# Left halves of three normalized residuals turned by transposing DMAs instead of TensorE

## The chip, the cores and the metric

The kernel runs on one core of a Trainium2 chip. The metric is the time of one execution in device microseconds (us); the time before is the median of three runs. The engines are named as in the profile: PE (TensorE, matrix products and transposes), PEld (its weight loads), DVE (VectorE), ACT (ScalarE), POOL (GpSimd) and SP (SyncE, which only issues DMAs here).

## The reference

One decoder layer on 256 tokens of width 2048, in float32. `h` is the residual stream:

```
h = h + 0.5 * swiglu(rmsnorm(h, g_ffn1), w1_gate, w1_up, w1_down)      # "f1", width 5632
z = rmsnorm(h, g_mix) @ w_in                                           # q, kv, v, u
y = concat(rmsnorm(spatial_gating(z)), rmsnorm(window_attention(z)))
h = h + y @ w_out                                                      # "wo"
h = h + cross_attention(rmsnorm(h, g_x), rmsnorm(mem, g_mem), ...)     # "xq", ..., "xo"
h = h + 0.5 * swiglu(rmsnorm(h, g_ffn2), w2_gate, w2_up, w2_down)      # "f2"
return rmsnorm(h, g_final)

def rmsnorm(x, g):
    return x * rsqrt(mean(x * x) + 1e-5) * g
```

Three of these norms stand between a product that adds into `h` and the next product: n2 (g_mix), n3 (g_x) and n4 (g_ffn2). They are the ones that change.

## The kernel before

**Products.** `h` lies by rows: 256 tokens are two blocks of 128 partitions, and the 2048 columns are four parts (j = 0 to 3) of 512. A product with a weight matrix needs the left operand turned, so that the 128 partitions hold columns. For this the columns are cut into eight pairs of 128 columns each; pair i holds two column blocks by two token blocks, a tile of 128 x 512. The "left half" of a norm is parts j = 0 and 1, pairs 0 to 3.

Each float32 product is done in three passes: an operand is split into a high half (a cast on ACT, line 147) and a low half (the rest, a subtraction on DVE, line 148), and PE multiplies high by high, low by high and high by low (line 411). Products of 2 x 2 blocks are done in a form with seven products instead of eight; the kinds "C", "S" and "D" of a pair say which sums and differences of its blocks `fill` makes on DVE (the tiles named f, for instance n2f).

**Units and chunks.** A unit is one product of all pairs with 1024 columns of a weight matrix; it runs chunk by chunk, one pair with one megabyte of weights each. `load` brings the weights by SP (three buffers for what comes in, two for the halves) and splits them: f1dw, f1dwh and f1dwl are the weights of the unit f1d, their high and their low half. Kind "S" also makes sums of weight blocks (f1dt).

**The order.** PE runs in the order in which the program is written. The other engines' instructions are put in order by a scheduler when the kernel is built; on the chip each engine takes its list strictly in that order. Small work beside the products is written as generators in the list `side`: after every sixth matmul `side_step` lets one of them go on, and the number that a generator yields is how many such steps it then rests.

**The norms.** `next_norm` returns `on_block`, which the unit that adds into `h` calls for each block that is done. The squares of a block are summed on ACT (line 137, output junk). When the left half is there, an estimated factor from its squares scales the rows (`scaled`, line 822, tile n2s, n3s or n4s); the right parts are scaled by the same factor once they are done, after the last chunk of the unit. `make` then turns pair after pair: `transposed` makes four PE transposes into a PSUM bank (tile n, line 231), two ACT instructions per pair read the bank and multiply by the norm's gain g (line 249, tile n2r), and `fill` makes the differences and the halves (n2fh, n2fl). Its generators rest 4 steps before the first pair of a part and 1 before the second.

**Additions into h.** A unit of wo or xo ends with a group of additions on DVE (lines 610 to 624, early sums, and 604, the last four). They stand between the low halves of the last chunks in DVE's list.

**A way of turning that is already there.** In the feed-forward parts the rows are turned without PE: `rows_done` copies the rows on ACT so that the low and the high halfwords of the floats lie apart (line 661, tile f1w), SP issues a transposing DMA on 16-bit elements (line 665, tile f1a), and `joined` puts the halfwords together again, two ACT copies per pair (line 679, tile f1r).

Of the kernel before, what the change touches and what calls it, by code (L numbers as in the profile page):

```python
# [10 lines left out]
U16 = mybir.dt.uint16  # L11
AF = mybir.ActivationFunctionType
# [3 lines left out]
P = 128  # L16
T = 256
TB = 2
# [15 lines left out]
def layer_kernel(  # L34
# [22 lines left out]
    nc = tc.nc  # L57
# [26 lines left out]
    sm = const.tile([P, N_SMALL], F32, name="sm")  # L84
# [34 lines left out]
    h = const.tile([P, TB, D], F32, name="h")  # L119


    def rstd_of(parts, n, width, nt=TB):

        ss = tiny.tile([P, nt], F32, tag="ss", name=nm("ss"))
        if n > 1:
            nc.vector.tensor_reduce(out=ss, in_=parts, axis=AX.X, op=ALU.add)
        else:
            ss = parts.rearrange("p t n -> p (t n)")
        ms = tiny.tile([P, nt], F32, tag="ms", name=nm("ms"))
        nc.vector.tensor_scalar(ms, ss, 1.0 / width, EPS, op0=ALU.mult, op1=ALU.add)  # L130
        rs = tiny.tile([P, nt], F32, tag="rs", name=nm("rs"), bufs=8)
        nc.gpsimd.tensor_tensor(rs, ms, mhalf[:, :nt], ALU.pow)
        return rs

    def square_into(parts_ap, src, width):
        junk = s2("junk")
        nc.scalar.activation(junk[:, :width], src, AF.Square, accum_out=parts_ap)

    def split_scaled(hi, lo, src, g):

        nc.scalar.activation(hi, src, AF.Copy, scale=g)
        nc.vector.scalar_tensor_tensor(
            out=lo, in0=src, scalar=g, in1=hi.bitcast(F32), op0=ALU.mult, op1=ALU.subtract
        )

    def split(hi, lo, src):
        nc.scalar.copy(hi, src)  # L147
        nc.vector.tensor_tensor(lo, src, hi.bitcast(F32), ALU.subtract)  # L148

    def products(o, passes):  # L150
        for i, (a, b) in enumerate(passes):
            nc.tensor.matmul(o, a, b, start=i == 0, stop=i == len(passes) - 1)
# [49 lines left out]
    def fill(s, p, raw):  # L202

        f = s2(s + "f").rearrange("p (k t) -> p k t", k=4)
        if p.kind == "C":
            f = f[:, :2, :]
            nc.vector.tensor_tensor(f, raw[:, 0:2, :], raw[:, 2:4, :], ALU.subtract)
        elif p.kind in "SD":
            nc.vector.tensor_tensor(
                f[:, 0:2, :], raw[:, 0:1, :].to_broadcast([P, 2, P]), raw[:, 1:3, :], ALU.subtract  # L210
            )
        split(p.base[0], p.base[1], raw)
        if p.kind in "SD":
# [12 lines left out]
    def transposed(s, kind, src):  # L226

        ps = bank(s).rearrange("p (k t) -> p k t", k=4)
        for k in range(2):
            for tb in range(TB):  # L230
                nc.tensor.transpose(ps[:, laid(kind, k, tb), :], src(tb, k), ident)
        return ps

    def row_tile(kind, v, k):

        return v[:, k::2, :] if kind == "C" else v[:, 2 * k:2 * k + 2, :]

    def pair_from_rows(s, kind, src, gcol):
        ps = transposed(s, kind, src)
        p = Pair(s, kind)  # L240
        if kind != "N":
            raw = s2(s + "r").rearrange("p (k t) -> p k t", k=4)
        for k in range(2):
            g = sm[:, gcol + k:gcol + k + 1]
            if kind == "N":
                hi, lo = [row_tile("N", t, k) for t in p.base]
                split_scaled(hi, lo, row_tile("N", ps, k), g)
            else:
                nc.scalar.activation(row_tile(kind, raw, k), row_tile(kind, ps, k), AF.Copy, scale=g)
        if kind != "N":  # L250
            fill(s, p, raw)
        return p
# [171 lines left out]
    def side_add(gen):  # L424
        side.append([now[0], gen])
# [226 lines left out]
    def ffn(s, get, rs, wgu, wd, on_block, first=None, on_token_block=None):  # L652
        acts = [None] * 22
        pairs = [None] * 22

        def rows_done(c, rows_):
            turned_ = m4(s + "a").bitcast(U16).rearrange("p (b c t) -> p b c t", b=TB, c=8)

            def turned(tb):
                w = s2(s + "w").bitcast(U16)  # L660
                nc.scalar.copy(
                    w.rearrange("p (h c) -> p h c", h=2),
                    rows_[tb].bitcast(U16).rearrange("p (c h) -> p h c", h=2),
                )
                nc.sync.dma_start_transpose(turned_[:, tb], w)
                for q in range(2):
                    acts[2 * c + q] = turned_

            for tb in range(TB):
                later.append((tb, lambda tb=tb: turned(tb)))  # L670

        def joined(i):
            turned_ = have(acts, i).rearrange("p b (h c) t -> p b c t h", h=2)
            raw = s2(s + "r")
            words = raw.bitcast(U16).rearrange("p (i t h) -> p i t h", i=4, h=2)
            q = 2 * (i % 2)
            for tb in range(TB):
                j, k = laid(KINDS_D[i], 0, tb), laid(KINDS_D[i], 1, tb)
                nc.scalar.copy(words[:, j:k + 1:k - j], turned_[:, tb, q:q + 2])
            return raw.rearrange("p (i t) -> p i t", i=4)  # L680
# [76 lines left out]
        for n, idx in enumerate(turns):  # L757
            half = n % 2
            kinds = "".join(KINDS_D[i] for i in idx)
# [28 lines left out]
    def next_norm(s, gcol, kinds="NNNNNNNN"):  # L788

        mixed = "S" in kinds
        parts = tiny.tile([P, TB, NG], F32, tag="parts", name=nm("parts"))
        pairs = [None] * 8
        done = [0] * NG
        st = {}

        def on_block(j, tb):  # L800
            square_into(parts[:, tb, j:j + 1], h[:, tb, j * 512:(j + 1) * 512], 512)
            done[j] += 1
            if not mixed:
                if done[j] == TB:
                    make(j, lambda tb, c: h[:, tb, c:c + P])
            elif j < 2:
                if done[0] + done[1] == 2 * TB:
                    st["est"] = rstd_of(parts[:, :, :2], 2, 1024)

                    def first():  # L810
                        yield 1
                        for i in range(2):
                            scaled(i)

                    side_add(first())
            elif done[j] == TB:
                scaled(j)

        def scaled(j):
            r = m4(s + "s").rearrange("p (b c) -> p b c", b=TB)  # L820
            for tb in range(TB):
                nc.scalar.activation(
                    r[:, tb], h[:, tb, j * 512:(j + 1) * 512], AF.Copy, scale=st["est"][:, tb:tb + 1]
                )
            make(j, lambda tb, c: r[:, tb, c - j * 512:c - j * 512 + P])

        def make(j, src):
            def work():
                for i in (2 * j, 2 * j + 1):
                    yield 4 if i % 2 == 0 and mixed else 1  # L830
                    pairs[i] = pair_from_rows(
                        s, kinds[i], lambda tb, k: src(tb, (2 * i + k) * P), gcol + 2 * i
                    )

            side_add(work())

# [531 lines left out]
    for j in range(2):  # L1368
        g = m4("gf")
# [123 lines left out]
```

## Time and profile before

| | us |
|---|---|
| median of the runs | 2039.45 (2039.23, 2039.45, 2040.15) |
| the profiled execution | 2038.53 |
| its span, first to last instruction | 2036.8 |
| PE busy | 2019.8 (99%) |
| DVE busy | 1858.2 (91%) |
| ACT busy | 1297.9 (64%) |
| mean granted clock of PE | 0.998 |

The profile is of one execution, so sums over its rows are compared with 2038.53 and not with the median. Times in a trace are counted from the start of the span. The f1d unit ends and q begins near 701; wo ends and xq begins near 1138; xo ends and f2g begins near 1342. A row of a timeline gives start, length, engine, line, operation, output<-input; in brackets stands how long the engine was idle before and what released it. "x2" joins equal neighbours.

### The profile page before, as it was taken

To read this page: it belongs to the slowest core of one execution; us is meant where nothing else is said; L and a number is where in the kernel's file an instruction comes from. 1 tells how busy PE (TensorE), PEld (TensorE's weight loads), DVE (VectorE), ACT (ScalarE), POOL (GpSimd) and SP (SyncE) were. 2 spreads that over 40 slices of the span, in tenths; PEclk is the share of its full clock that TensorE was granted. 3 is DMA by queue.
4 is the path that set the end of the run, shared out by engine and by line. 5 is a ranking of instruction groups with operands and counts; after the bars stand their busy time and mean duration, and the time that the engine had idled before them with its cause. 6 is when DMAs were issued, how large, how long until landed. Compare 5 with 4: busy or idle time off the path is not lost.

```text
span 2036.8 us, 24300 instructions
## 1 busy us (share of the span) xinstructions
PE 2019.8 (99%) x9235; PEld 1671.6 (82%) x9235; DVE 1858.2 (91%) x1998; ACT 1297.9 (64%) x1432; POOL 36.3 (2%) x57
## 2 busy tenths in 40 slices
PE   9999999999999999999999999999999999999998
PEld 8788888888888888888888888888888888888886
DVE  6999999999999978988988987899999999999998
ACT  7865656567665766655556655675656666676664
POOL 0000000000000010100000000000000000000000
PEclk9999999999999999999999999999999999999999
DMA  8666666666555565545555544556566656665563
GB/s 312 195 209 232 214 219 197 232 217 218 204 192 205 187 243 176 196 166 183 193 182 179 198 161 145 186 186 218 199 234 210 217 213 225 220 215 209 186 225 127
DMA packets 106884, 413.72 MB, mean 203 GB/s; under 512 B 53376, under 2 KB 55440, under 8 KB 59664
## 3 DMA queue, kind: packets, MB, share of 16 engines
q1 hardware_dynamic: 104320, 405.04, 57.5%
q0 software_dynamic: 2016, 6.30, 0.9%
q8 instruction: 72, 1.18, 0.2%
q10 hardware_dynamic: 432, 0.84, 0.1%
q14 instruction: 44, 0.36, 0.1%
HBM read 398.52 MB, written 2.10 MB: 197 GB/s over the span
## 4 chain that ended last, share of the span: by engine, by line
PE 85%; DVE 8%; issue 3%; ACT 1%; DMA 1%; SPq 0%; POOL 0%; POOLq 0%; DVEq 0%; ACTq 0%
PE f2gQ L411 13%; PE f1gQ L411 12%; PE f2dQ L411 6%; PE f1dQ L411 6%; PE f1gP L411 5%; PE f2gP L411 4%; PE xqQ L411 3%; PE f2dP L411 3%; PE f1dP L411 3%; PE woQ L411 2%; PE xoQ L411 2%; PE f2dR L411 2%; PE f1dR L411 2%; DVE f1gwl L148 2%; PE vQ L411 2%
## 5 line engine op out<-in xcount | busy, mean ns | idle before, releaser
L148 DVE TENSOR_TENSOR f1gwl<-f1gw,f1gwh 128x1536 fp32r<-128x1536 f32 (+2 forms) x94 | 181.6, 1934 | 23.3 <-ACT f1gwh L147 22.4
L147 ACT CAST f2gwh<-f2gw 128x1536 fp32r<-128x1536 f32 (+1 forms) x88 | 150.3, 1711 | 59.6 <-PE f2gQ L411 39.2
L148 DVE TENSOR_TENSOR f2gwl<-f2gw,f2gwh 128x1536 fp32r<-128x1536 f32 (+1 forms) x88 | 179.2, 2037 | 9.6 <-ACT f2gwh L147 9.6
L147 ACT CAST f1gwh<-f1gw 128x1536 fp32r<-128x1536 f32 (+2 forms) x94 | 153.0, 1629 | 44.4 <-PE f1gQ L411 18.0
L147 ACT CAST f1gth<-f1gt 128x1024 fp32r<-128x1024 f32 x76 | 79.9, 1051 | 102.7 <-DVE f1gt L320 67.7
L147 ACT CAST f2gth<-f2gt 128x1024 fp32r<-128x1024 f32 x82 | 85.9, 1049 | 69.7 <-DVE f2gt L324 40.4
L411 PE MATMUL f2gQ<-f2gwh,n4fh 128*128 128x512 f32 x317 | 124.2, 392 | 1.5 <-DVE f2gv L570 1.5
L411 PE MATMUL f2gQ<-f2gwh,n4fl 128*128 128x512 f32 x317 | 123.4, 389 | 0.0
L411 PE MATMUL f1gQ<-f1gwh,n1fl 128*128 128x512 f32 x286 | 111.4, 390 | 1.7 <-DVE n1fl L148 1.7
L411 PE MATMUL f1gQ<-f1gwh,n1fh 128*128 128x512 f32 x286 | 111.6, 390 | 0.0
L147 ACT CAST f2dwh<-f2dw 128x2048 fp32r<-128x2048 f32 (+1 forms) x44 | 77.4, 1759 | 47.5 <-PE f2dQ L411 39.5
L147 ACT CAST f1dwh<-f1dw 128x2048 fp32r<-128x2048 f32 (+1 forms) x44 | 77.3, 1757 | 43.7 <-PE f1dQ L411 42.7
L148 DVE TENSOR_TENSOR f1dwl<-f1dw,f1dwh 128x2048 fp32r<-128x2048 f32 (+1 forms) x44 | 92.0, 2091 | 11.3 <-ACT f1dwh L147 11.2
L148 DVE TENSOR_TENSOR f2dwl<-f2dw,f2dwh 128x2048 fp32r<-128x2048 f32 (+1 forms) x44 | 92.1, 2092 | 11.2 <-ACT f2dwh L147 11.1
L148 DVE TENSOR_TENSOR f2gtl<-f2gt,f2gth 128x1024 fp32r<-128x1024 f32 x82 | 99.7, 1219 | 1.0
L411 PE MATMUL f2gQ<-f2gwl,n4fh 128*128 128x512 f32 x317 | 96.7, 389 | 0.0
L148 DVE TENSOR_TENSOR f1gtl<-f1gt,f1gth 128x1024 fp32r<-128x1024 f32 x76 | 92.2, 1217 | 0.5
L411 PE MATMUL f1gQ<-f1gwl,n1fh 128*128 128x512 f32 x286 | 86.9, 389 | 0.0
L411 PEld LDWEIGHTS f2gQ<-f2gwh,n4fh 128*128 128x128 f32 x317 | 59.5, 188 | 15.9 <-DVE f2gv L570 3.7
L411 PEld LDWEIGHTS f2gQ<-f2gwl,n4fh 128*128 128x128 f32 x317 | 59.4, 188 | 12.3
L411 PEld LDWEIGHTS f2gQ<-f2gwh,n4fl 128*128 128x128 f32 x317 | 59.5, 188 | 12.1
L411 PE MATMUL f2gP<-f2gwh,n4fh 128*128 128x512 f32 x176 | 68.6, 390 | 0.0
(823 smaller groups left out, 6057.8 us busy)
## 6 DMA issues: line engine op xcount, KB each, us to landing
f2gw<-in_w_gu SPq DMA_DIRECT2D x88, 1024.0 KB, 5.1
f1gw<-in_w_gu SPq DMA_DIRECT2D x86, 1024.0 KB, 4.9
f1dw<-in_w_down SPq DMA_DIRECT2D x44, 1024.0 KB, 4.8
f2dw<-in_w_down SPq DMA_DIRECT2D x44, 1024.0 KB, 4.8
wow<-in_w_out SPq DMA_DIRECT2D x16, 1024.0 KB, 4.8
xqw<-in_w_xq SPq DMA_DIRECT2D x16, 1024.0 KB, 4.8
xow<-in_w_xo SPq DMA_DIRECT2D x16, 1024.0 KB, 4.8
qw<-in_w_in SPq DMA_DIRECT2D x8, 1024.0 KB, 4.8
```

What stands on the lines that cost most here:

```text
L147: nc.scalar.copy(hi, src)
L148: nc.vector.tensor_tensor(lo, src, hi.bitcast(F32), ALU.subtract)
L411: nc.tensor.matmul(self.banks[name], x, y, start=name not in self.begun, stop=self.left[name] == 0)
```

## The change

For parts j = 0 and 1 of n2, n3 and n4 the scaled rows are turned in the way of the feed-forward parts. `turned_rows` is called once for each of the two token blocks: one ACT copy of 128 x 1024 halfwords (n2w) and one transposing DMA on SP into n2t; four of each per norm. `pair_joined` takes the place of `pair_from_rows` for pairs 0 to 3: two ACT copies of halfwords from n2t into n2r, two ACT multiplications by g that read and write n2r, then `fill` as before. The generators now rest 6 steps before the first pair of a part and 3 before the second. Parts 2 and 3, and the norms of the feed-forward parts, stay as they are; the hunk that is left out only moves lines of `rows_done` and `joined` into the new helper functions.

```
--- before.py
+++ after.py
@@ -147,6 +147,23 @@
         nc.scalar.copy(hi, src)
         nc.vector.tensor_tensor(lo, src, hi.bitcast(F32), ALU.subtract)
 
+    def turned_rows(s, dst, src):
+
+        w = s2(s + "w").bitcast(U16)
+        nc.scalar.copy(
+            w.rearrange("p (h c) -> p h c", h=2), src.bitcast(U16).rearrange("p (c h) -> p h c", h=2)
+        )
+        nc.sync.dma_start_transpose(dst, w)
+
+    def tile_turned(s):
+        return m4(s).bitcast(U16).rearrange("p (b c t) -> p b c t", b=TB, c=8)
+
+    def by_block(turned):
+        return turned.rearrange("p b (h c) t -> p b c t h", h=2)
+
+    def words_of(raw, n):
+        return raw.bitcast(U16).rearrange("p (i t h) -> p i t h", i=n, h=2)
+
     def products(o, passes):
         for i, (a, b) in enumerate(passes):
             nc.tensor.matmul(o, a, b, start=i == 0, stop=i == len(passes) - 1)
@@ -247,6 +264,27 @@
                 split_scaled(hi, lo, row_tile("N", ps, k), g)
             else:
                 nc.scalar.activation(row_tile(kind, raw, k), row_tile(kind, ps, k), AF.Copy, scale=g)
+        if kind != "N":
+            fill(s, p, raw)
+        return p
+
+    def pair_joined(s, kind, turned, c, gcol):
+
+        raw = s2(s + "r")
+        words = words_of(raw, 4)
+        for tb in range(TB):
+            j, k = laid(kind, 0, tb), laid(kind, 1, tb)
+            nc.scalar.copy(words[:, j:k + 1:k - j], by_block(turned)[:, tb, c:c + 2])
+        raw = raw.rearrange("p (k t) -> p k t", k=4)
+        p = Pair(s, kind)
+        for k in range(2):
+            g = sm[:, gcol + k:gcol + k + 1]
+            src = row_tile(kind, raw, k)
+            if kind == "N":
+                hi, lo = [row_tile("N", t, k) for t in p.base]
+                split_scaled(hi, lo, src, g)
+            else:
+                nc.scalar.activation(src, src, AF.Copy, scale=g)
         if kind != "N":
             fill(s, p, raw)
         return p
...
@@ -822,7 +855,20 @@
                 nc.scalar.activation(
                     r[:, tb], h[:, tb, j * 512:(j + 1) * 512], AF.Copy, scale=st["est"][:, tb:tb + 1]
                 )
-            make(j, lambda tb, c: r[:, tb, c - j * 512:c - j * 512 + P])
+            if j < 2:
+                t = tile_turned(s + "t")
+                for tb in range(TB):
+                    turned_rows(s, t[:, tb], r[:, tb])
+
+                def work():
+                    for q in range(2):
+                        yield 6 if q == 0 else 3
+                        i = 2 * j + q
+                        pairs[i] = pair_joined(s, kinds[i], t, 2 * q, gcol + 2 * i)
+
+                side_add(work())
+            else:
+                make(j, lambda tb, c: r[:, tb, c - j * 512:c - j * 512 + P])
 
         def make(j, src):
             def work():
```

The change moves instructions on ACT and DVE. Three places follow, each before and then now; a number behind a name only tells the tiles of one name apart.

ACT, the end of f1d, where the left half of n2 is scaled. Before:

```order
L147 CAST f1dwh_5246<-f1dw_5245 128x2048
L822 ACTIVATE n2s_5267<-h,rs_5243 128x512 x2
L822 ACTIVATE n2s_5270<-h,rs_5243 128x512 x2
L147 CAST f1dwh_5286<-f1dw_5285 128x1536
L147 CAST f1dth_5299<-f1dt_5289 128x1024
```

and now (line 822 has become 855):

```order
L147 CAST f1dwh_5246<-f1dw_5245 128x2048
L855 ACTIVATE n2s_5267<-h,rs_5243 128x512 x2
L153 COPY n2w_5271<-n2s_5267 128x1024
L153 COPY n2w_5274<-n2s_5267 128x1024
L855 ACTIVATE n2s_5277<-h,rs_5243 128x512 x2
L153 COPY n2w_5281<-n2s_5277 128x1024
L153 COPY n2w_5284<-n2s_5277 128x1024
L147 CAST f1dwh_5300<-f1dw_5299 128x1536
```

Four copies to n2w stand between the scaled rows and the cast of f1d's next weights.

ACT, the end of f1d and the start of q (n2r_5465, n2r_5486 and n2r_5511 are the joined pairs 0, 2 and 1; n2t_5270 holds pairs 0 and 1, n2t_5280 pairs 2 and 3). Before:

```order
L822 ACTIVATE n2s_5583<-h,rs_5243 128x512
L137 ACTIVATE junk_5575,parts_118<-h 128x512
L137 ACTIVATE junk_5578,parts_118<-h 128x512
L137 ACTIVATE junk_5581,parts_118<-h 128x512
L822 ACTIVATE n2s_5583<-h,rs_5243 128x512
L137 ACTIVATE junk_5587,parts_118<-h 128x512
L822 ACTIVATE n2s_5589<-h,rs_5243 128x512 x2
L147 CAST n2fh_5516<-n2f_5521 128x512
L147 CAST qwh_5593<-qw_5592 128x2048
L147 CAST qwh_5631<-qw_5630 128x2048
```

and now:

```order
L147 CAST n2fh_5470<-n2f_5474 128x256
L277 COPY n2r_5486<-n2t_5280 128x512
L147 CAST qwh_5595<-qw_5594 128x2048
L287 ACTIVATE n2r_5486<-n2r_5486,sm 128x2x128 x2
L147 CAST qth_5748<-qt_5742 128x1024
L147 CAST n2fh_5489<-n2r_5486 128x512
L147 CAST qwh_5633<-qw_5632 128x2048
L147 CAST n2fh_5470<-n2f_5493 128x256
L277 COPY n2r_5511<-n2t_5270 128x512 x2
L147 CAST qth_5752<-qt_5742 128x1024
L287 ACTIVATE n2r_5511<-n2r_5511,sm 128x2x128 x2
L147 CAST n2fh_5514<-n2r_5511 128x512
```

Pairs 0 to 3 were made ahead of the first of these rows before, except for one cast of pair 3. Now the last scaled rows (n2s) stand ahead of the first row shown, pair 2 is joined before pair 1, and pair 1's high half (n2fh_5514) is the last row, behind two casts of q's weights.

DVE, the end of wo. Before:

```order
L148 TENSOR_TENSOR wowl_9116<-wow_9114,wowh_9115 128x2048
L621 TENSOR_TENSOR h<-h,wop_1818_9141 128x512
L148 TENSOR_TENSOR wowl_9155<-wow_9153,wowh_9154 128x2048
L611 SCALAR_TENSOR_TENSOR wov_9142<-woQ_1806_9050,wop_1818_9141 128x512
L604 SCALAR_TENSOR_TENSOR h<-woQ_1804_9048,h 128x512
L614 SCALAR_TENSOR_TENSOR woz_9143<-woQ_1805_9049,wov_9142 128x512
L604 SCALAR_TENSOR_TENSOR h<-woQ_1804_9048,h 128x512
L622 TENSOR_TENSOR h<-h,wov_9142 128x512
L623 TENSOR_TENSOR h<-h,woz_9143 128x512
L624 TENSOR_TENSOR h<-h,woz_9143 128x512
```

and now (lines 604, 611, 614 and 621 to 624 have become 642, 649, 652 and 659 to 662):

```order
L148 TENSOR_TENSOR wowl_9088<-wow_9086,wowh_9087 128x2048
L649 SCALAR_TENSOR_TENSOR wov_9114<-woQ_1798_9022,wop_1810_9113 128x512
L642 SCALAR_TENSOR_TENSOR h<-woQ_1796_9020,h 128x512
L652 SCALAR_TENSOR_TENSOR woz_9115<-woQ_1797_9021,wov_9114 128x512
L642 SCALAR_TENSOR_TENSOR h<-woQ_1796_9020,h 128x512
L659 TENSOR_TENSOR h<-h,wop_1810_9113 128x512
L660 TENSOR_TENSOR h<-h,wov_9114 128x512
L661 TENSOR_TENSOR h<-h,woz_9115 128x512
L662 TENSOR_TENSOR h<-h,woz_9115 128x512
L148 TENSOR_TENSOR wowl_9127<-wow_9125,wowh_9126 128x2048
```

The low half of wo's last chunk (wowl_9155, now wowl_9127) stood in front of seven additions and now stands behind them. At the end of xo the low half of the last chunk has moved in the same way, behind eight additions and two rows of pair 2 of n4; and on ACT the loading of a function table (line 93) has moved from before the last squares of n4 to just before the cast of f2g's second chunk.

More of the change, by code (lines that the diff above doesn't have):

```diff
@@ L656, in rows_done @@
         def rows_done(c, rows_):
-            turned_ = m4(s + "a").bitcast(U16).rearrange("p (b c t) -> p b c t", b=TB, c=8)
+            t = tile_turned(s + "a")
             def turned(tb):
[L660 to L665, printed above, removed]
+                turned_rows(s, t[:, tb], rows_[tb])
                 for q in range(2):
-                    acts[2 * c + q] = turned_
+                    acts[2 * c + q] = t
             for tb in range(TB):
@@ L672, in joined @@
         def joined(i):
-            turned_ = have(acts, i).rearrange("p b (h c) t -> p b c t h", h=2)
+            turned_ = by_block(have(acts, i))
             raw = s2(s + "r")
-            words = raw.bitcast(U16).rearrange("p (i t h) -> p i t h", i=4, h=2)
+            words = words_of(raw, 4)
             q = 2 * (i % 2)
```

## The prediction

> **What bounds the kernel now.** I read the busy shares and the chain of waits first.
>
> ```profile
> PE 2019.8 (99%) x9235; PEld 1671.6 (82%) x9235; DVE 1858.2 (91%) x1998; ACT 1297.9 (64%) x1432; POOL 36.3 (2%) x57
> PE 85%; DVE 8%; issue 3%; ACT 1%; DMA 1%; SPq 0%; POOL 0%; POOLq 0%; DVEq 0%; ACTq 0%
> ```
>
> PE sets the time: 2019.8 of 2036.8 us. So a transpose taken from PE is worth its length, and work given to ACT (64% busy) looks free. These are averages over stages, though. Next I read what PE waits for, and the chain of waits where f1d ends and q begins:
>
> ```profile
> PE f1gQ L411 <- DVE n1fl L148: 1.7, 1, 1.7
> ...
> PE xoQ L411 <- ACT n4r L249: 1.2, 1, 1.2
> ```
>
> ```profile
> 692.82 0.44 PE n L231 x4
> ...
> 694.23 1.93 ACT qwh L147
> ...
> 703.50 1.23 ACT n2s L822 x2
> ...
> 707.10 1.20 PE qP L411 x4
> ```
>
> PE waits once for 1.7 us and once for 1.2 (columns: in total, times, longest), and no DMA stands among its waits. But at the junction the chain leaves PE: from 694 to 707 it runs over ACT and DVE. ACT's load there:
>
> ```profile
> 700.00:720.00 20.00, 19.81 (x96) 16.10 (x95) 19.03 (x31) 20.00 (x37) 5.46 (x7) 1.00 0.64 228
> 1095.00:1165.00 70.00, 70.00 (x326) 57.97 (x325) 64.59 (x79) 51.71 (x73) 2.24 (x2) 1.00 0.53 183
> ```
>
> (Columns after the window: its length, then busy us of PE, PEld, DVE, ACT, POOL; then the granted clock.) For 20 us at the start of q ACT is busy all the time. That is where the change puts work on it. The next junction (wo to xq, second row) has room on ACT, 51.71 of 70, but DVE is 92% busy; the third (xo to f2g) is built like it.
>
> **What is removed.** Twelve groups of four transposes, four groups in each of three norms. A group costs PE 0.44 us in the chain above: 12 x 0.44 = **-5.3 us**, all on PE's path. One sentence of the Trainium skill bears on that price. Its page "VectorE: DVE Perf Modes", section "The three transpose paths", gives a 128x128 TensorE transpose 390 ns; taken as a pitch, 48 of them would be -18.7 and the sum below near no change, but the trace puts four in 0.44, so the trace's price stands.
>
> **What is added on ACT.** Per norm four copies that sort halfwords (128x1024) and eight that join a pair (128x512). The first trace shows the same forms in the feed-forward part. In scaling, eight instructions that read PSUM become eight that read SBUF; that form is not shown, so I keep L249's length, and as bounds 0.1 less or more each, 0.8 a norm.
>
> ```profile
> L661 ACT COPY f1w<-f1gz 128x1024 uint16<-128x1024 uint16 x10 | 10.4, 1041 | 0.0
> L679 ACT COPY f1r<-f1a 128x512 uint16<-128x512 uint16 x44 | 27.7, 680 | 0.0
> 709.99 0.82 ACT L249 ACTIVATE n2r<-n,sm 128x256 f32<-128x256 f32 x2
> ```
>
> Successive ACT instructions overlap: two of L249 take 0.82, and a cast of 1.04 is followed 0.95 later by the next (the rows of 710.71 and 711.65 below). I take 0.95 for the first copy and 0.63 for the second: 4 x 0.95 + 8 x 0.63 = 8.8 us of ACT per norm, 26.5 in all. What matters is what stands behind them.
>
> **Junction 1a, in f1d.** The four large copies stand before the cast of an f1d chunk (first place shown of the change).
>
> ```profile
> 669.33 1.46 ACT L147 CAST f1dwh<-f1dw 128x1536 fp32r<-128x1536 f32 x1
> 670.83 1.76 DVE L148 TENSOR_TENSOR f1dwl<-f1dw,f1dwh 128x1536 fp32r<-128x1536 f32 x1 [2.19 <-ACT f1dwh L147]
> ...
> 674.93 0.40 PE L411 MATMUL f1dP<-f1dwl,f1afh 128*128 128x512 f32 x1
> ```
>
> The cast moves from 669.33 to 673.1, its end to 674.6, the low half's end to 676.4. PE, two transpose groups earlier, wants it at 674.93 - 0.88 = 674.05. **+2.4.** Queued behind are the other f1d casts, which have room: two L249 pairs are gone there. With all four groups of n2 gone (1.76), PE is then 0.65 late.
>
> **Junction 1b, q's second chunk.** The pairs come in the order 0, 2, 1, 3, so pair 1, which PE needs second, stands behind pair 2's rows and two casts of q's weights (second place shown).
>
> ```profile
> 701.51 0.69 DVE L604 SCALAR_TENSOR_TENSOR h<-f1dQ,h 128x512 f32<-128x512 f32 x1
> 701.31 0.39 PE L411 MATMUL qP<-qwh,n2fh 128*128 128x512 f32 x1
> 705.14 3.72 ACT L147 CAST qwh<-qw 128x2048 fp32r<-128x2048 f32 x2
> 710.71 1.04 ACT L147 CAST qth<-qt 128x1024 fp32r<-128x1024 f32 x1
> 711.65 0.62 ACT L147 CAST n2fh<-n2r 128x512 fp32r<-128x512 f32 x1
> ...
> 711.83 1.22 DVE L148 TENSOR_TENSOR qtl<-qt,qth 128x1024 fp32r<-128x1024 f32 x1
> ```
>
> The last addition into h ends at 702.20 and now at 702.85; the last scaled rows follow it (0.71) to 703.6. Then ACT does, in the new order, at these lengths less the overlap: 0.31 + 0.63 + 1.86 + 0.74 + 0.95 + 0.53 + 1.86 + 0.31 + 1.26 + 0.95 + 0.74 + 0.62 = 10.8. Pair 1's high half is there at 714.4. PE starts q at 701.31 + 0.65 and ends its first chunk, 24 matmuls at 0.227, at 707.4. **+7.0.** (A cast of 128x256 I put at half of one of 128x512.) Pair 1's low half stands on DVE behind the low half qtl (1.22), some **+1.3** more; the gap that stood there before, from 706.75 to the 707.10 of the chain, is inside the new one: **-0.35**. Junction 1: **+10.4**.
>
> **Junctions 2 and 3, the last wo and xo chunks.** There DVE makes the chunk's low half after the additions into h instead of before (third place shown).
>
> ```profile
> L231 PE MATMUL n<-ident,n3s x16: 270/272/273, 1103.4 to 1109.2; 128*128 128x128 f32 x16
> ...
> 1126.49 2.28 DVE L148 TENSOR_TENSOR wowl<-wow,wowh 128x2048 fp32r<-128x2048 f32 x1
> 1128.69 0.68 DVE L611 SCALAR_TENSOR_TENSOR wov<-woQ,wop 128x512 f32<-128x512 f32 x1
> 1132.29 0.68 DVE L624 TENSOR_TENSOR h<-h,woz 128x512 f32<-128x512 f32 x1
> 1132.93 0.39 PE L411 MATMUL woP<-wowl,ybfh 128*128 128x512 f32 x1
> 1330.70 2.28 DVE L148 TENSOR_TENSOR xowl<-xow,xowh 128x2048 fp32r<-128x2048 f32 x1
> 1337.07 0.39 PE L411 MATMUL xoP<-xowl,xofh 128*128 128x512 f32 x1
> ```
>
> Seven additions from 1128.69 are 7 x 0.60 = 4.2 us; the low half, ready at 1128.77, had 4.16 of room. So the order alone takes all the room and no more. DVE is late by more: PE skips the four groups of the first row (16 transposes up to 1109.2), 1.8 us, ahead of this place, while DVE has the same rows to do. With 0.4 for the copies I take **+2.3** (0 to 4.7: nothing, or 0.9 and the full 3.8 of the large copies on top). For xo two rows of pair 2 (0.28 and 0.6) stand in front too: 5.0 + 2.2 - 4.1 = **+3.1** (0 to 5.6).
>
> Then the next unit's second chunk. Its cast on ACT stands behind the squares and the scaled rows:
>
> ```profile
> 1135.69 0.67 DVE L604 SCALAR_TENSOR_TENSOR h<-woQ,h 128x512 f32<-128x512 f32 x1
> 1137.66 0.61 ACT L137 ACTIVATE junk<-h 128x512 f32<-128x512 f32 x1
> 1140.76 1.89 ACT L147 CAST xqwh<-xqw 128x2048 fp32r<-128x2048 f32 x1
> ...
> 1330.36 1.28 ACT L93 ACT_TABLE_LOAD   x1
> ...
> 1344.94 1.90 ACT L147 CAST f2gwh<-f2gw 128x2048 fp32r<-128x2048 f32 x1
> ...
> 1347.50 0.39 PE L411 MATMUL f2gP<-f2gwh,n4fh 128*128 128x512 f32 x1
> ```
>
> In the new order three scaled rows (0.61 each, as in the chain), four squares (0.62), the last scaled row (0.62) and a cast of the joined pair 3 (0.53) follow the second addition into h and stand before the cast: 5.5 us, where it was 4.4 (1136.36 to 1140.76), so +1.1. The additions themselves stand behind two low halves (2 x 2.2), two small rows (0.9) and each other (2 x 0.6), 6.6 from the start of the late low half, and by PE's own count from there (2.3 + 22 x 0.227 + 24 x 0.227 = 12.7) end 6.1 ahead of the need; before it was 7.0 (the need is 1132.93 + 46 x 0.227 = 1143.37), so +0.9. Room was 0.7 (the cast ended at 1142.65). xq: **+1.3.** f2g also gets the table load, 1.28 + 0.2, which lay in idle time at 1330 and now stands right before the cast: 2.4 + 0.9 - 0.7 = **+2.6.** Behind that I expect one more wait in f2g, since all of ACT's rows behind that cast come 2 to 3 late, **+1.0** (0 to 2). The wait of xoQ for n4r over PSUM goes away: **-1.2.**
>
> **The sum:** 10.4 + 2.3 + 1.3 + 3.1 + 2.6 + 1.0 - 1.2 - 5.3 = +14.2. The profiled execution took 2038.53 (span 2036.8), so 2052.7; the median of the runs, 2039.45, is 0.9 above it: **2053.5 us**.
>
> **The transposing DMAs** I cost at nothing. On SP's queue four stand among f1d's loads, each issued when its copy is done (to 673.1).
>
> ```profile
> f1a<-f1w SPq DMA_TRANSPOSE x22, 3.2
> ...
> 672.62 5.29 SPq L341 DMA_DIRECT2D f1dw<-in_w_down  x2
> 683.09 1.92 ACT L147 CAST f1dwh<-f1dw 128x2048 fp32r<-128x2048 f32 x1 [1.01 <-PE f1dQ L411]
> f1dw<-in_w_down SPq DMA_DIRECT2D x44, 1024.0 KB, 4.8
> ```
>
> The load issued at 672.62 lands 4.8 later, at 677.4, and its cast comes at 683.09: 5.7 of room hide a delay of some 2 to 5 us. Without that cover a junction loses up to the 3.2 of one transpose, some 2 us beyond the room each.
>
> **Rivals.** (a) *The clock.* After a gap of 7 us PE could come back slower; the trace shows PE coming out of rest only at its start:
>
> ```profile
> 1.12 5.06 PE L98 MATMUL warm<-ones 128*128 128x128 f32 x22 [1.12 <-DVE ones L89]
> ```
>
> 22 matmuls in 5.06 us are 0.23 each, against 0.11 for a transpose of the same size in the groups of 0.44. So half pace for 5 us is possible, up to +2.5: 2056. For it: this row. Against: the other waits (at most 1.7) show nothing. Chance 0.30. The Trainium skill says in "TensorE: Matmul & The Clock Gate", section "What's actually happening", that an idle window of about 3.4 us halves the clock and as long a busy one restores it; by its figures the loss would be an estimated 1.7, and no wait of the trace before is long enough to show it.
>
> (b) *Faster.* ACT and DVE take the rows in stride. The mechanism: pair 1 ready before PE's second q chunk. It decides at 707.4 - 703.6 = 3.8 us of ACT rows between the last scaled rows and pair 1; the order has 10.8. If the engines reached these rows early enough, only -5.3 and -1.2 remain: 2033. It would take the order at run time to be other than the built one. Chance 0.06.
>
> (c) *SP's queue holds the weights up.* Four transposes of 3.2 in line, each waiting for ACT, and the loads of 4.8 behind them late in all three junctions: 3 x 2 more, 2060. For: SP issues in order. Against: the 5.7 of room, and the 22 such transposes of f1 without a DMA in PE's waits. Chance 0.08.
>
> (d) *Half of it.* Junctions 2 and 3 keep their room (DVE starts the additions earlier) and only junction 1 costs: 10.4 - 5.3 - 1.2 = +3.9, 2043. Chance 0.11. My forecast keeps 0.45.
>
> **How the numbers follow.** The likeliest case by its own bounds is 2053.5 with 2047 to 2059: down 2.3, 3.1 and 1.0 with every open cost at its lower end; up 2.4, 2.5 and 1.0. The clock adds 2.5; (d) ends at 2043. Range 2044 to 2061, which leaves out (b) and part of (c) and (d). A difference below 0.2%, 4 us, is no change. Faster only with (b), 0.06; within 0.2% for the lower part of (d), 0.06; slower 0.88.
>
> **What would show it.** No transposes of n3 between 1103 and 1110, where 16 stand now, and the like for n2 and n4. In PE's waits a new row of about 7 us, q's second chunk waiting for n2fh, then one of 1.3 for n2fl; one of 2 to 3 each for wowl and xowl; one for xqwh and one of 2.5 for f2gwh. ACT busy up by about 26. If the first q chunk is followed without a gap, junction 1 is wrong, and with it the forecast; if the gaps are there and the time is the same, the -5.3 was mis-sized. Matmul pitch above 0.227 right after the 7 us gap would show (a); PE waits on a DMA would show (c).

## The result and the profile after

The changed kernel takes **2061.51 us** (median of four runs, 2060.75 to 2061.90); the kernel before, timed beside it, 2039.34. The ratio is 1.0111 (95% interval 1.0098 to 1.0123): 22 us slower. The prediction was slower by 14, 2053.5, with a range of 2044 to 2061. The direction held, and so did the places that it named; the size did not, and the result lies just outside the range.

The profiled execution took 2061.13 us with a span of 2059.2 (before 2038.53 and 2036.8). Its busy time, on the page:

```profile
PE 2022.3 (98%) x9187; PEld 1669.1 (81%) x9187; DVE 1859.0 (90%) x1998; ACT 1323.0 (64%) x1468; POOL 33.9 (2%) x57
```

48 matmuls fewer, and yet PE is busy 2.5 us longer than before: work was taken away, and what is left goes slower. ACT is busy 25 us longer, as reckoned (26.5). What PE waits for (in total, times, longest):

```profile
PE qP L449 <- ACT n2fh L147: 6.6, 1, 6.6
PE xoP L449 <- DVE xowl L148: 4.7, 2, 2.9
PE woP L449 <- DVE wowl L148: 2.7, 2, 2.3
...
PE f2gQ L449 <- ACT f2gth L147: 1.4, 1, 1.4
PE f2gP L449 <- ACT f2gwh L147: 1.4, 1, 1.4
...
PE f1dP L449 <- DVE f1dwl L148: 1.1, 1, 1.1
PE qP L449 <- DVE qwl L148: 1.0, 1, 1.0
```

Nearly every row is one that the prediction named. xowl and wowl stand there twice each, where one of each was forecast, and qwl was not forecast. Behind the wait of 6.6, in the timeline of PE:

```profile
707.44 0.39 PE L449 MATMUL qQ<-qwl,n2fh 128*128 128x512 f32 x1
714.47 0.79 PE L449 MATMUL qP<-qwh,n2fh 128*128 128x512 f32 x1 [6.64 <-ACT n2fh L147]
716.08 0.80 PE L449 MATMUL qP<-qwh,n2fl 128*128 128x512 f32 x1 [0.82 <-DVE n2fl L148]
716.67 0.63 PE L449 MATMUL qP<-qwh,n2fh 128*128 128x512 f32 x1
717.10 0.63 PE L449 MATMUL qP<-qwh,n2fl 128*128 128x512 f32 x1
...
718.38 1.05 PE L248 MATMUL n<-ident,n2s 128*128 128x128 f32 x4
...
720.69 0.39 PE L449 MATMUL qQ<-qwh,n2fh 128*128 128x512 f32 x1
720.92 0.40 PE L449 MATMUL qQ<-qwh,n2fl 128*128 128x512 f32 x1
```

From 716.67 to 720 a matmul follows the last after 0.43 us; from 720.5 on after 0.23. The windows give the clock with it (the number after POOL's):

```profile
714.00:720.00 6.00, 4.71 (x12) 3.52 (x13) 3.93 (x9) 5.93 (x16) 1.15 (x2) 0.50 0.48 183
720.00:726.00 6.00, 6.00 (x33) 4.93 (x32) 2.13 (x6) 3.71 (x8) 1.02 (x1) 0.97 0.27 79
1147.00:1150.00 3.00, 2.31 (x10) 1.93 (x11) 3.00 (x4) 1.93 (x5) 0.00 (x0) 1.00 0.40 112
1355.00:1358.00 3.00, 2.89 (x7) 2.31 (x8) 3.00 (x4) 2.51 (x5) 0.00 (x0) 0.55 0.61 180
```

After the gap at q the clock is 0.50, after the wait of 2.3 at the end of wo (third row) 1.00, after the wait of 2.9 at the end of xo (last row) 0.55.

The 9187 matmuls of the changed kernel all stand in the kernel before too, in the same order, so the start of each can be compared. PE's lateness, matmul by matmul, adds up as follows (us, in the two profiled executions):

| where | predicted | measured |
|---|---|---|
| twelve transpose groups | -5.3 | -4.4 (0.36 each) |
| f1d, chunk behind the large copies | +2.4 | +1.9 |
| q, second chunk (n2fh, n2fl) | +8.0 | +7.3 |
| wo, last chunk | +2.3 | +2.4 |
| xq, second chunk | +1.3 | +1.2 |
| xo, last chunk | +3.1 | +3.1 |
| f2g, second chunk | +2.6 | +1.6 |
| f2g, one more wait | +1.0 | +1.6 |
| xo's wait for n4r gone | -1.2 | -1.3 |
| **these together** | **+14.2** | **+13.4** |
| half clock behind q's gap | (rival a) | +2.6 |
| half clock behind xo's gap | none | +1.8 |
| q's third chunk, low half | none | +1.2 |
| wo, two earlier chunks | none | +1.6 |
| xo, an earlier chunk | none | +1.9 |
| **in all** | **+14.2** | **+22.5** |

The two profiled executions differ by 22.6, so these rows leave next to nothing over.

### The profile page after: what moved, and what is told of

Same layout as the page of the kernel before. It is cut to its first block, busy times and chain, and to the rows that moved or that the text cites. A ratio compares the mean times of both kernels' runs of the same rounds, so it can differ in the third digit from the quotient of the medians.

```text
span 2059.2 us, 24261 instructions
## 1 busy us (share of the span) xinstructions
PE 2022.3 (98%) x9187; PEld 1669.1 (81%) x9187; DVE 1859.0 (90%) x1998; ACT 1323.0 (64%) x1468; POOL 33.9 (2%) x57
## 4 chain that ended last, share of the span: by engine, by line
PE 72%; issue 15%; DVE 8%; ACT 3%; DMA 1%; POOL 0%; SPq 0%; POOLq 0%; DVEq 0%; ACTq 0%
PE f2gQ L449 13%; PE f1gQ L449 11%; PE f2dQ L449 6%; PE f2gP L449 5%; PE f1gP L449 4%; PE xqQ L449 3%; PE f2dP L449 3%; PE f2dR L449 2%; DVE f1gwl L148 2%; PE xoQ L449 2%; PE vQ L449 2%; PE mv0Q L449 2%; PE mv1Q L449 2%; PE mk1Q L449 1%; PE mk0Q L449 1%
## 5 line engine op out<-in xcount | busy, mean ns | idle before, releaser
L148 DVE TENSOR_TENSOR f2dwl<-f2dw,f2dwh 128x2048 fp32r<-128x2048 f32 (+1 forms) x44 | 92.1, 2092 | 11.0 <-ACT f2dwh L147 10.6
```

## The experiments

**1. Is the slow stretch the clock?** PE is kept busy in the gap at q:

```
+KEEP = 27
...
+    def keep_busy():
+        kps = bank("keep")
+        for i in range(KEEP):
+            nc.tensor.matmul(kps[:, :P], ones, ones, start=True, stop=True)
...  (called ahead of q's second chunk)
```

> The changed kernel with 27 matmuls of ones by ones (about 6.2 us at full pace, nobody reads the result) between q's first and second chunk, where PE waits 6.6 us for the high half of pair 1. Theory: the wait ends at the same time, but PE's clock does not fall, so the matmuls behind it go at 0.227 us instead of 0.43: granted clock 1.00 there, 2.5 to 3.0 us less, 2058.5 to 2059.0. Rival (the slow matmuls come from operands that are late, not from the clock): no change, 2061.5, and pitch of 0.4 stays.

Measured: 2058.82 us, ratio 1.0096 (1.0082 to 1.0110), 2.7 less than the change. The trace has the filler as 54 matmuls in 6.19 us and not as 27: the function was called twice. The intervals of the two ratios overlap, so the time alone is weak; the windows say more:

```profile
676.00:680.00 4.00, 3.39 (x8) 2.72 (x9) 4.00 (x4) 2.02 (x2) 0.00 (x0) 0.59 1.35 223
709.00:716.00 7.00, 6.45 (x56) 6.18 (x54) 7.00 (x8) 6.97 (x11) 0.00 (x0) 1.00 0.41 150
716.00:721.00 5.00, 3.83 (x11) 2.93 (x12) 3.47 (x7) 4.93 (x14) 1.01 (x2) 0.67 0.57 213
```

While the filler runs the clock is 1.00. The two short waits that are left behind it (0.6 for n2fh, 1.1 for n2fl) still bring a shorter slow stretch. The first row is f1d, where in this execution the waits of 0.9 and 1.1 were followed by one too, though not in the changed kernel's. So the slow matmuls are the clock's and follow from idle PE, not from operands; 1.00 throughout, as expected, was not reached. Nor does the clock explain the 2.7 us: in this execution it is at half for 3.4 us in f1d, 3.4 at q and 6.8 at the end of xo, together as long as in the changed kernel (10.2 at q, 3.4 at xo).

**2. What is the removal worth by itself?** The transposes go, nothing comes:

```
-        ps = transposed(s, kind, src)
+        ps = transposed(s, kind, src) if flat is None else None
...
-                nc.scalar.activation(row_tile(kind, raw, k), row_tile(kind, ps, k), AF.Copy, scale=g)
+                src = row_tile(kind, ps, k) if flat is None else flat[:, :, k * P:(k + 1) * P]
+                nc.scalar.activation(row_tile(kind, raw, k), src, AF.Copy, scale=g)
```

> The kernel before without the twelve groups of transposes and with nothing in their place: pairs 0 to 3 of n2, n3 and n4 are scaled by ACT straight from the unturned rows, so these left operands are wrong and the turn is left out. The prediction's term: the transposes stand on PE's path, -5.3 to -6.5, so 2033 to 2034. Theory now: around the junctions DVE's and ACT's lists set the pace, and PE only waits longer for them (about 1.6 for qwl, 1.9 for wowl, 2.5 in xo): within 1 us of before, 2038.5 to 2040.5.

Measured: 2039.55 us, ratio 1.0006 (0.9997 to 1.0015). **The removal is worth nothing.** PE is busy 4 us less (2015.8) and waits as much more:

```profile
PE xoQ L412 <- DVE xotl L148: 2.3, 1, 2.3
...
PE woP L412 <- DVE wowl L148: 1.5, 1, 1.5
...
PE qP L412 <- DVE qwl L148: 1.4, 1, 1.4
```

Each group gives its 0.36 us, and each junction takes it back: PE is 1.4 us early behind the groups of n2 and waits 1.6 longer at q, 1.4 early behind those of n3 and 1.7 later at wo, and the like at xo. PE gets to the low half of the weights earlier, and DVE makes it when it did before. Of the 28 us up to the end of wo DVE is busy 27.06 before and 26.88 here. The built order is another one too, so part of these waits may be the order's.

**3. Is it the order of the pairs?** The rests of before, so that the pairs come as 0, 1, 2, 3:

```
-                        yield 6 if q == 0 else 3
+                        yield 4 if q == 0 else 1
```

> The changed kernel with the rests of before (4 and 1 steps instead of 6 and 3), so that the joined pairs come in the order 0, 1, 2, 3 and earlier. Rival (the rests and the order 0, 2, 1, 3 are the cause): the wait of 6.6 at q's second chunk and the slow clock behind it go, and nothing comes instead: about 2051. Theory (the cause is the work put on ACT and DVE at these places, whatever its order): the wait at q shrinks to 1 or 2 and others grow, in f1d, and before xq's and f2g's second chunks (3 to 5 each): 2057 to 2061.

Measured: 2059.04 us, ratio 1.0101 (1.0087 to 1.0115). The wait for n2fh is gone, and others have come:

```profile
PE xqP L449 <- DVE xqwl L148: 4.5, 1, 4.5
PE xoP L449 <- DVE xowl L148: 4.1, 3, 2.5
PE f2gP L449 <- DVE f2gwl L148: 2.8, 1, 2.8
PE f1dP L449 <- DVE f1dwl L148: 2.1, 2, 1.1
```

The longest wait has moved from q to xq. The order decides where the time is lost, hardly how much.

**4. One norm at a time.**

```
-            if j < 2:
+            if j < 2 and s == "n2":      (and the same for "n3" and "n4")
```

> The change for n2 alone. Theory: each junction pays by itself. From the lateness of PE in the changed kernel: f1d +1.9, q's second chunk +6.5 and +0.9, the half clock behind it +2.9, q's third chunk +1.2, four transpose groups -1.5: +11.9, about 2051. Rival (the junctions are not independent, a later one gives back what an earlier one lost): under 2047 or over 2055.

> The change for n3 alone. Theory: wo's chunks +1.0, +0.6 and +2.4, xq's second chunk +1.2, four transpose groups -1.5: +3.7, about 2042.7, and no half clock, since no wait reaches 2.5 us. Rival as for n2: the same as before or over 2046.

> The change for n4 alone. Theory: xo's chunks -1.3, +1.9 and +3.1, the half clock behind the last +1.9, f2g's chunks +1.6 and +1.6, four transpose groups -1.5, and half a us more or less in f2g: +6.8, about 2045.8. With n2 and n3 the three add up to 22. Rival: the three add up to under 17 or over 27.

Measured: n2 alone 2048.18 (ratio 1.0042, 1.0028 to 1.0057), n3 alone 2043.22 (1.0020, 1.0010 to 1.0029), n4 alone 2049.55 (1.0047, 1.0032 to 1.0062). Against the kernel before beside them, 2038.94, that is +9.2, +4.3 and +10.6, together 24.1 where the change costs 22: the junctions pay each by itself. n2 came 3 below its expectation and n4 4 above. In the profile of n2 alone PE is 12.0 late behind q, as expected (11.9). In that of n4 alone the clock is at half for 6.8 us behind xo, not 3.4, which costs 3.0 instead of 1.9; and a chunk of xo waits 1.1 for xowh, whose cast stands in ACT's list behind a wait of 2.5 for a transposing DMA (n4t).

**5. The first half of the change beside the old turn.** The twelve large copies and the transposing DMAs are done, TensorE still turns, nobody reads what the DMAs bring:

```
             if j < 2:
                 t = tile_turned(s + "t")
                 for tb in range(TB):
                     turned_rows(s, t[:, tb], r[:, tb])
-                def work(): ...
-            else:
-                make(j, ...)
+            make(j, lambda tb, c: r[:, tb, c - j * 512:c - j * 512 + P])
```

> The kernel before (TensorE turns, rests of 4 and 1 steps) with the first half of the change beside it: the twelve 128x1024 copies on ACT and the twelve transposing DMAs are done, and nobody reads what they turn. No joins, no change of what PE does. Theory (a few us of ACT ahead of the casts are enough, since DVE behind it has no room): waits of 1 to 3 us in f1d, wo and xo for the halves of the weights (f1dth, woth, xoth), together +10 to +13, about 2051. Rival (the joins are the cause, the first copies are hidden): 2039 to 2042. Rival (the DMAs are the cause): a DMA row among PE's or ACT's waits that holds most of the loss.

Measured: 2058.60 us, ratio 1.0093 (1.0078 to 1.0108): 20 us, more than expected, while ACT is busy 9.2 us longer than before (1307.1).

```profile
PE xoQ L449 <- ACT n4r L266: 3.6, 2, 1.8
PE f2gQ L449 <- DVE f2gv L608: 3.1, 5, 0.9
PE woQ L449 <- ACT n3r L266: 2.7, 1, 2.7
```

PE now waits for ACT to empty the banks in which it turned n3 and n4: the copies stand in front of that reading. No DMA is among the waits. The first copies are far from hidden. Not all of the 20 us are lost at the junctions: the clock falls to half twice (for 3.4 us in wo and 6.8 in xo), and in the profiled execution 4 to 5 us go in f2g after 1480, for a reason that stays open.

**6. Without the large copies, and without the joins.** In the one, ACT writes the scaled rows as 16-bit halves into a cleared tile and the DMA turns that; in the other ACT scales what lies in the turned tile:

```
-                    turned_rows(s, t[:, tb], r[:, tb])
+                    nc.sync.dma_start_transpose(t[:, tb], r[:, tb].bitcast(U16))
...  (and the scaling into a tile that POOL has cleared)
```

```
-            nc.scalar.copy(words[:, j:k + 1:k - j], by_block(turned)[:, tb, c:c + 2])
...
-                nc.scalar.activation(src, src, AF.Copy, scale=g)
+                nc.scalar.activation(src, flat[:, :, 4 + 2 * k:6 + 2 * k, :].rearrange("p b c t -> p b (c t)"), AF.Copy, scale=g)
```

> The changed kernel without its twelve 128x1024 copies: ACT writes the scaled rows as 16-bit halves with zeros between them (POOL clears the tile ahead), and the DMA turns that tile as it is, so the left operands of pairs 0 to 3 are wrong; the sorting of halfwords is left out. DMAs, joins and rests as in the change. If the parts add up (without joins 2056.4, so the joins are 5 of 22): 2044 to 2046. Theory (each part alone is enough to make ACT's list late where it matters; the joins alone still put pair 1 behind pair 2 and two casts at q): no wait in f1d, but 6 to 7.5 for n2fh at q, 3 in xo and 2.5 and 1.6 in f2g: 2049 to 2054.

> The changed kernel without the 24 joining copies: ACT scales from the turned tile what stands there as halfwords (the left operands of pairs 0 to 3 are wrong; the joining is left out). Large copies, transposing DMAs and rests as in the change. Theory (joins and large copies share the loss, the joins most of the wait at q): the wait of 6.6 at q's second chunk shrinks to 2 or less and its half clock goes, those of f1d, wo and xo stay at 2 to 3 each: 2049 to 2055. Rival (the large copies do it all, as in the run with the turn beside): 2058 or more.

Measured: without the large copies 2056.75 (ratio 1.0092, 1.0077 to 1.0107), without the joins 2056.38 (1.0085, 1.0071 to 1.0098). Against the kernel before beside them that is +18.9 and +18.3, so either half of ACT's new work left out takes only 3 to 4 of the 22 us off. **They do not add up; each is enough.** Without the large copies f1d's wait is gone, and q's is as long as ever and xo's longer:

```profile
PE qP L450 <- ACT n2fh L148: 7.0, 1, 7.0
PE xoP L450 <- DVE xowl L149: 5.7, 2, 4.2
```

In this run it is not the amount of work that makes pair 1 late at q: ACT stands idle for 3.81 us, waiting for DVE's h, just ahead of the rows of pair 1 in its list. Without the joins the same time goes in waits of 1 to 3 us for qwl, qwh, wotl and xowl. So both came out slower than expected: the first lies 3 above the 2049 to 2054 of the theory, and far above the 2044 to 2046 by addition; the second lies 1 above its range.

**7. The large copies later, one by one:**

```
                 def work():
+                    for tb in range(TB):
+                        yield 1
+                        turned_rows(s, t[:, tb], r[:, tb])
                     for q in range(2):
-                        yield 6 if q == 0 else 3
+                        yield 3 if q == 0 else 1
```

> The whole change, with its large copies issued later and one by one (one step of side work apart, then rests of 3 and 1 before the joins) instead of all four behind the scaled rows. Rival (the place of the copies ahead of f1d's cast is what costs): the 1.9 in f1d and the 6.5 at q with its slow clock go and nothing comes: about 2050. Theory (the same work has to be done by ACT and DVE before q, wo and xo end, so it comes out elsewhere): f1d and q's second chunk without a wait, 2 to 3 each in q's later chunks, wo, xq, xo and f2g: 2055 to 2059.

Measured: 2054.68 us, ratio 1.0086 (1.0069 to 1.0103): the fastest version of the whole change. f1d and q's second chunk wait no more; q's later part does (4.2 for n2r), wo 2.7, xo 2.2, f2g 2.9. That is 17 us more than the kernel before beside it, where the change costs 22.

**8. The copies on POOL.**

```
-            nc.scalar.copy(words[...], by_block(turned)[:, tb, c:c + 2])
+            nc.gpsimd.tensor_copy(words[...], by_block(turned)[:, tb, c:c + 2])
...  (and the same in turned_rows for n2, n3 and n4)
```

> The changed kernel with its 36 halfword copies (both kinds) on POOL, which is 2% busy, instead of ACT. Theory (ACT's list is what is late): if a copy takes POOL no more than 2 us, the waits for n2fh and for the late low halves go, and the time comes down to what is without transposes, 2039 to 2045. Rival (the transposing DMAs or DVE's order make the lateness): 2055 or more. If POOL takes 4 us or more for a copy the pairs come late for another reason, which its rows will show: over 2060.

Measured: 2062.53 us, ratio 1.0119 (1.0104 to 1.0135). ACT is back at 1297.6 us, and nothing is won. POOL's groups and one row of ACT:

```profile
L277 POOL COPY n4r<-n4t 128x512 uint16<-128x512 uint16 x8 | 12.5, 1584 | 11.9 <-DVE n4fl L148 6.3 <-DMA n4t<-n4w 5.6
...
L153 POOL COPY n4w<-n4s 128x1024 uint16<-128x1024 uint16 x4 | 9.0, 2291 | 1.2 <-ACT n4s L855 1.2
```

```profile
680.66 1.49 ACT L147 CAST f1dwh<-f1dw 128x1536 fp32r<-128x1536 f32 x1 [5.36 <-DMA f1dw<-in_w_down]
```

A large copy takes POOL about twice as long as ACT (2.29 against 1.04). The small ones vary: the mean of 1.58 above hides a median of 0.67, as on ACT, and one copy of 7.68. PE now waits 5.9 for n2fl, and ACT waits for POOL's n3r and n4r, so the pairs are late again. Here the transposing DMAs wait on SP for POOL and hold back f1d's weights, so that ACT stands idle for 5.4 us; PE does not wait for them. ACT's load is thus not the only way to this loss.

**9. Relief for DVE.** Four additions into h that read SBUF only go from DVE to POOL, in three kernels: without transposes, before, and the change.

```
             def rest():
-                nc.vector.tensor_tensor(hb(0, 0), hb(0, 0), p1, ALU.add)
+                eng.tensor_tensor(hb(0, 0), hb(0, 0), p1, ALU.add)
...  (and the three below it; eng is nc.gpsimd in units that add into h)
```

> The kernel without the twelve groups of transposes (left operands of pairs 0 to 3 unturned, as in the run without transposes), and the four additions into h that read SBUF only (lines 622 to 624 and 621 of before, in f1d's last two units, wo and xo) moved from DVE to POOL. Theory (the 5.3 us were there, but DVE's full list took them back at the junctions): the waits for qwl, wowl and xotl go and the time falls by the price of the transposes, 2033.5 to 2035.5. Rival (the transposes were never on the path): no change, 2038.5 to 2040.5. If POOL takes over 2.5 us for an addition, h comes late: over 2040.

> The kernel before with the same four additions on POOL and nothing else. Theory: PE has almost no wait there to win (0.35 at q), since its transposes give DVE the time it needs: the same as before, 2038 to 2040. Rival (relief of DVE is worth something by itself): 2037 or less.

> The changed kernel with the same four additions on POOL. Theory: the late low halves of wo and xo (2.4, 1.9, 3.0 with the half clock) mostly go, since the additions no longer stand before them; the wait of 6.6 for n2fh, which is ACT's, stays: 2050 to 2054. Rival (the lateness is all ACT's): 2060 or more. If it falls under 2042, DVE's additions were the whole cause.

Measured: 2038.27 (ratio 0.9996, 0.9988 to 1.0005), 2044.48 (1.0025, 1.0016 to 1.0034) and 2063.44 (1.0116, 1.0095 to 1.0136). All three expectations failed: no gain, a loss of 5 to 6, no gain. The move is no pure relief. POOL's addition takes up to 6.3 us while DVE works, and a low half on DVE beside it 1.78 instead of 0.68:

```profile
685.91 6.32 POOL L624 TENSOR_TENSOR h<-h,f1dp 128x512 f32<-128x512 f32 x1 [13.91 <-ACT f1dp L611]
692.36 1.29 POOL L625 TENSOR_TENSOR h<-h,f1dv 128x512 f32<-128x512 f32 x1
...
693.61 1.48 POOL L627 TENSOR_TENSOR h<-h,f1dz 128x512 f32<-128x512 f32 x1
```

```profile
693.86 1.78 DVE L148 TENSOR_TENSOR n2fl<-n2r,n2fh 128x512 fp32r<-128x512 f32 x1
...
702.58 0.68 DVE L148 TENSOR_TENSOR n2fl<-n2r,n2fh 128x512 fp32r<-128x512 f32 x1
```

In the first of the three the theory half shows: PE is 3.5 us ahead of before at 1365, early in f2g. It has lost nearly all of it by 1593, waiting in f2g for f2gwl (1.3) and f2gtl (0.9). DVE is 97 to 98 us busy in each 100 there in the kernel before:

```profile
1480.00:1580.00 100.00, 100.00 (x441) 81.88 (x440) 97.53 (x89) 59.92 (x50) 0.00 (x0) 1.00 0.65 225
1580.00:1680.00 100.00, 99.62 (x439) 81.62 (x438) 97.80 (x94) 62.80 (x54) 0.00 (x0) 1.00 0.61 213
```

So even a lead that gets past the junctions finds an engine with 2 to 3% of room behind it.

## Why the prediction was right in direction and short in size

**Right.** "At the junction the chain leaves PE" was the reading that carried it. The terms that it led to measured 13.4 together where 14.2 was forecast, and each of the large ones within 1 us: f1d 1.9 for 2.4, q 7.3 for 8.0, wo 2.4 for 2.3, xo 3.1 for 3.1. The prices held too: large copies follow each other after 0.95, two joins take 1.25, scaling from SBUF takes 0.90 for a pair of instructions where 0.82 was kept. A transpose group was put at 0.44 and is worth 0.36. (The last step of the sum, 2039.45 and 14.2, gives 2053.6 and not 2053.5.)

The result is 8 us above the forecast, and two terms that the sum put at nothing account for it: the slow clock with 4.4 and the earlier chunks with 4.7. The terms that were forecast came out 0.8 lower together.

**Wrong, the clock.** It was rival (a), at a chance of 0.30 and 2.5 us for one gap. It came, at 2.6 there, and once more behind xo's wait of 2.9 with 1.8. The step that failed is "the other waits (at most 1.7) show nothing" as evidence against it: they were too short to tell. It belonged in the forecast.

What decides is not the length of a wait. In each of the sixteen traces the clock changes only at instants that lie a whole number of steps of 3.41 us apart; in the changed kernel it falls at 710.17 and 1355.29. From 20 to 2000 us of these traces, half clock followed on every step at full clock in which PE was idle for 1.98 us or more (22 steps), on none with less than 1.69, and on two of the fifteen between. The wait of 2.3 at wo is split by the end of a step, that of 2.9 at xo is not. The two steps, in columns as above:

```profile
1143.71:1147.12 3.41, 1.73 (x8) 1.11 (x6) 3.41 (x4) 2.51 (x3) 0.00 (x0) 1.00 0.29 123
1351.88:1355.29 3.41, 0.49 (x3) 0.18 (x2) 3.41 (x4) 1.52 (x2) 0.00 (x0) 1.00 0.00 0
```

PE is idle for 1.7 us of the first and for 2.9 of the second. The Trainium skill's page "TensorE: Matmul & The Clock Gate", section "What's actually happening", has the mechanism, a free-running window of about 3.4 us. The traces agree with that length; its rule of one idle window before the clock falls, read as a window that is idle throughout, does not fit them, since 1.98 us of idle time in it sufficed.

**Wrong, the earlier chunks.** "Queued behind are the other f1d casts, which have room" was looked at for f1d, and for wo and xo only the last chunk was. 4.7 us stand in chunks ahead of it (wo +1.6, xo +1.9) and in q's third (+1.2), where the sum had nothing. In the changed kernel's windows ACT is busy 19.65 of 21 us ahead of xo's end and DVE 20 of 20 ahead of wo's:

```profile
1132.00:1152.00 20.00, 17.29 (x75) 13.66 (x75) 20.00 (x25) 15.70 (x23) 0.00 (x0) 1.00 0.57 209
1324.00:1345.00 21.00, 19.24 (x84) 15.07 (x82) 16.48 (x21) 19.65 (x25) 0.00 (x0) 1.00 0.91 236
```

Two or three chunks' work is late in such a stretch, not one.

**Wrong, the transposing DMAs.** "The transposing DMAs I cost at nothing" failed in wo and in xo, and it is part of these 4.7 us. ACT takes its list in order; in wo it waits for a transposed tile, the cast of a chunk's weights stands right behind, and PE waits for that cast. In xo a transposing DMA lies on the chain that leads to the first late xowl:

```profile
1125.72 0.69 ACT L277 COPY n3r<-n3t 128x512 uint16<-128x512 uint16 x1 [2.29 <-DMA n3t<-n3w]
1126.31 1.90 ACT L147 CAST wowh<-wow 128x2048 fp32r<-128x2048 f32 x1
1128.26 0.50 PE L449 MATMUL woP<-wowh,ybfh 128*128 128x512 f32 x1 [0.84 <-ACT wowh L147]
```

```profile
1323.83 7.32 DMA n4t<-n4w
```

The wait in wo makes PE 1.0 us later. With n3 alone ACT waits only 0.9 for n3t, and PE's wait for wowh is not there. How much of xo's 1.9 is the DMA's is not shown.

**Wrong, the credit.** "-5.3 us, all on PE's path" was the first term of the sum. In the change the groups are indeed 4.4 shorter, but experiment 2 shows that this buys nothing: the same room is asked back as waits. That term sat in the sum beside waits in which it was partly counted already (the 1.8 by which PE is early at wo), so the sum came out near for its parts; as a gain to be had it was not there. The argument from 99% busy to "a transpose taken from PE is worth its length" is the error.

**The other rivals.** Faster (b) and half (d) fell with the waits. SP's queue (c) did not come as it was told: no load of weights in f1d, wo or xo stands among ACT's waits, and no DMA among PE's. But the transposes landed after medians of 4.7 to 6.0 us instead of 3.2, ACT waited once each for n3t (2.3) and n4t (1.3), and PE waited behind ACT, as said.

**What stays open.** Every one of these kernels has its own built order on ACT and DVE. That the work on ACT is too much at these places and that its order is unlucky cannot be told apart fully: three orders of the whole change (experiments 3 and 7, and the change itself) cost 17 to 22, and half of the work 18 to 20. A version in which the lists are held fixed was not tried. Nor was one with the copies and without the transposing DMAs, so the share of the DMAs is known only from the waits; in experiment 5, where nobody waits for what they bring, the loss is 20 all the same. No run was faster than the kernel before by more than the noise.

## What to carry to other kernels

A stage in which PE is 99% busy can still be paced by a second engine with 2 to 8% of room: take the work out of PE alone first and see whether the time falls, before paying for it elsewhere. Price added work by the lists in which it stands and by every chunk behind it, not by the engine's mean share. Follow a late DMA through the engine that waits for it: what stands behind that wait in the engine's list is late too. Where a change opens gaps of 2 us or more on PE, count the slow clock behind them as likely.

## What the runs showed of the hardware that was not expected

- The granted clock changed only in steps of 3.41 us, and fell to half behind each step with 1.98 us or more of idle PE. A single wait of 2.2 us could bring it (the change with additions on POOL, xq) and one of 2.9 could fail to (experiment 7, f2g). In the changed kernel the slow stretches cost 1.8 and 2.6 us.
- POOL and DVE slow each other: an addition of 128x512 on POOL took 1.3 to 6.3 us, and a DVE row beside it 1.78 us instead of 0.68.
- A halfword copy of 128x1024 took POOL 1.0 to 2.6 us and ACT 1.04; one of 128x512 took POOL 0.66 to 7.7 us, with a median of 0.7 to 1.1 in each norm, and ACT 0.68.
- Transposing DMAs of the same size landed after a median of 3.2 us in the feed-forward parts and of 4.7 to 6.0 in f1d, wo and xo.
